# Ring tiles of 2560 instead of 2112 bytes for the left operands of a one-core decoder block, and six tiles of constants in a pool of their own

## The chip, the cores and the metric

The kernel runs on one core of one Trainium2 chip. The metric is device time in microseconds of one execution, the median of several runs. Five engines work side by side, each through its own list of instructions in order: TensorE (PE, with PEld for its weight loads), VectorE (DVE), ScalarE (ACT), GpSimd (POOL), and SyncE (SP), which issues the DMAs. They wait for each other through semaphores. SBUF is the on-chip memory from which the engines read; a tile takes the same stretch of bytes in each of 128 partitions. PSUM is where TensorE writes its sums.

## The reference

One layer of a decoder block on 1024 tokens of width 1024, in float32. What is computed, cut to what matters:

```
n    = rmsnorm(h, norm_mix)
proj = n @ w_in                      # z, xBC, dt, q, k, v, r, a1, g_ssd, g_gla: 7712 columns
y_s  = ssd_mixer(z, xBC, dt, ...)    # causal conv, chunked scan of 16 heads, gated norm
y_g  = gla_mixer(q, k, v, r, a1, ...)# gated linear attention, 4 heads, chunked
h    = h + (sigmoid(g_ssd) * (y_s @ w_up_ssd) + sigmoid(g_gla) * (y_g @ w_up_gla)) @ w_o
h    = h + cross_attention(rmsnorm(h, norm_xattn), rmsnorm(mem, norm_mem), w_xq, w_xkv, w_xo)
g, u = split(rmsnorm(h, norm_ffn) @ w_ffn_in)          # 2 x 2816 columns
h    = h + (silu(g) * u) @ w_ffn_out
out  = rmsnorm(h, norm_final)
```

## The kernel before

**Matrix products.** Each float32 operand of a large product is split into two float32r tiles, a high and a low part (`split`, L221: ACT copies to the high part, then DVE or POOL subtracts it). A product takes three matmuls per 128 rows of the contraction: high by high, high by low, low by high. Each such matmul loads 128 x 128 weights (the left, or stationary, operand) and streams 512 columns of the right, or moving, operand past them.

**Units.** The products with `w_in` and `w_ffn_in` are made in *units* of 256 columns (`Unit`, L275). A unit is one block product in the Strassen-Winograd form: seven products, named B11, B21, T1, B22, T2, T3 and T4, in place of eight. `Unit.step` (L320) makes one of the seven: it takes the left operand from the raw weights (`raw`) or a sum of them (`sa`), splits it into a pair of ring tiles `whi` and `wlo`, and issues 12 matmuls of 128 x 512 on them (L343, recorded at L51 in the helper), against the right operands `B11h`, `B11l` and so on, which hold the activations. There are 26 units on `w_in` and 22 on `w_ffn_in`: 48 x 7 x 12 = 4032 matmuls, in 21 groups of 192 by the names of their two operands.

**The ring.** `wring` (L225) gives out three pairs of tiles in turn, from the pool `wp`. Each tile holds 528 values of four bytes, 2112 bytes per partition. Of these, a unit uses 512 values: four slices (one for each k) of 128 values, so the slices are 512 bytes apart. Two other users need the ring. `kv_unit` (L549) makes keys and values of the memory tokens with 384 matmuls of 256 columns, and `v_steps` (L636) makes the columns for v, dt and a1 with 672 matmuls of 264 columns, where ring tiles are the moving operand.

**Slots.** The right operands, the raw weights and the results of units (`o`) live in *slots* of 8192 bytes: 14 in the pool `op`, 4 in `aux`, and later 4 in `m` (`open_slots`, L139). The four other large products take their left operand from a slot, too: `dense` (L1203) streams `hl` past `wd` with 1920 matmuls of 128 x 512, and the product with `w_ffn_out` (`piece`, L1596) streams `fs` past `fs`. `Att` multiplies `phl` and `kvhl`. None of these uses the ring.

**Where tiles lie.** A pool's tiles lie together. The pools opened for good lie in the order in which they are opened: constants (`cp`, L94), the ring (`wp`, L96), `op`, `aux`, and the sums `sa` (L148). Pools for a stage (`vp`, `gprep`, `conv`, `ssd`, `gla`) lie behind them, each in the place of the one that was closed. After the last of these is closed (L1133), `m`, `res` and `sa2` take their place. In the built program, the constants end at byte 9672 of the partition, the ring starts at 9696, the `op` slots at 22368, and the last tile of all ends at 229216.

**Order.** Each engine's list is fixed when the program is built. The units on `w_in` are interleaved, at rates written into the code (`run`, L438), with the steps of the SSD scan (`SSD`, L872) and then of the GLA scan (`GLA`, L1013), which are small float32 matmuls with work on ACT, DVE and POOL between them.

Of the kernel before, what the change touches and what calls it, by code (L numbers as in the profile page):

```python
# [9 lines left out]
F32 = mybir.dt.float32  # L10
F32R = mybir.dt.float32r
# [5 lines left out]
P = 128  # L17
# [4 lines left out]
MEM = 256  # L22
# [7 lines left out]
NCH = TOK // CH  # L30
NH = 16
# [47 lines left out]
def block_kernel(ctx: ExitStack, tc: tile.TileContext, t: dict, out: bass.AP):  # L79
# [10 lines left out]
    def pool(name, bufs=1, space=None, stack=None):  # L90
        kw = {"reuse_waits": "tile"} if space is None else {"space": space}
        return (stack or ctx).enter_context(tc.tile_pool(name=name, bufs=bufs, **kw))

    cp = pool("const")  # L94
    dr = pool("dram", 1, bass.MemoryType.DRAM)
    wp = pool("w", 3)  # L96
# [42 lines left out]
    def open_slots(key, n, stack):  # L139
        slots[key] = (pool(f"sl{len(slots)}{key}", n, stack=stack), n)  # L140
# [5 lines left out]
    open_slots("op", 14, opst)  # L146
    open_slots("aux", 4, auxst)
    sums = {"aux": pool("sa0", 2, stack=auxst)}  # L148

    st1 = ExitStack()  # L150
    vp = pool("vp", 1, stack=st1)
# [54 lines left out]
    def rsqrt(o, v, scale):  # L206

        DVE.tensor_scalar(o, v, scale, EPS, ALU.mult, ALU.add)
        POOL.tensor_tensor(o, o, mhalf[:, :o.shape[1]], ALU.pow)
# [13 lines left out]
        sub(e or DVE, lo, src, hi)  # L223

    def wring():  # L225
        hi = wp.tile([P, 528], F32R, name="whi", tag="whi", bufs=3)
        lo = wp.tile([P, 528], F32R, name="wlo", tag="wlo", bufs=3)
        return hi, lo

    class Operands:  # L230

# [43 lines left out]
    class Unit:  # L275
# [44 lines left out]
        def step(s, name, B, cs=ALL, again=False):  # L320
            s.load()
            kh = s.kh
            if name == "B11":
                s.banks, s.swap, s.u = {}, B.swap, False
                s.out()
            if again:
                wh, wl = s.w
            else:
                with ahead():
                    src = s.left(name)  # L330
                    hi, lo = wring()
                    s.w = wh, wl = [x[:, :kh * P].rearrange("p (k c) -> p k c", c=P) for x in (hi, lo)]
                    split(src, wh, wl)
            xh, xl = B[name]
            key = s.BANK[name]
            fresh = key not in s.banks
            if fresh:
                s.banks[key] = acc()
            p = s.banks[key]
            m = 0  # L340
            for k in range(kh):
                for x, y in ((wh, xh), (wh, xl), (wl, xh)):
                    PE.matmul(p[:, cs], x[:, k, :], y[:, k, cs], start=fresh and m == 0, stop=m == 3 * kh - 1,  # L343
                              skip_group_check=True)
                    m += 1
            s.evac(name, p, cs)
# [106 lines left out]
    def drain(g):  # L453
        for _ in g:
            pass
# [88 lines left out]
    for a in range(2):  # L544
        ACT.activation(msq, wide(mt[:, a]), AF.Square, accum_out=mss[:, a:a + 1])
    rsqrt(mss, mss, 1.0 / D)
    mbc = cp.tile([P, MEM], F32, name="mbc")

    def kv_unit(c0):  # L549

# [6 lines left out]
        for kk in range(4):  # L557
            with ahead():
                hi, lo = wring()
                hv = hi[:, :512].rearrange("p (k c) -> p k c", c=256)  # L560
                lv = lo[:, :512].rearrange("p (k c) -> p k c", c=256)
                split(raw[:, 2 * kk:2 * kk + 2, :], hv, lv, either(lo))
            for i in range(2):
                o = pa[i][:, :256]
                for k2 in range(2):
                    k = 2 * kk + k2
                    for m, (x, y) in enumerate(((hv, mh), (lv, mh), (hv, ml))):
                        w_, m_ = x[:, k2, :], y[:, k, :]
                        if c0 < D:
                            PE.matmul(o, w_[:, i * P:(i + 1) * P], m_, start=k == 0 and m == 0, stop=k == 7 and m == 2)  # L570
                        else:
                            PE.matmul(o, m_[:, i * P:(i + 1) * P], w_, start=k == 0 and m == 0, stop=k == 7 and m == 2)
            yield
# [41 lines left out]
    w_in = t["w_in"]  # L615


    dt_t = cp.tile([P, NCH, NH], F32, name="dt_t")
    a1_t = cp.tile([P, NCH, NH], F32, name="a1_t")
    HW = 264  # L620

    vraw = {}
# [13 lines left out]
    def v_steps():  # L636
        for pr in range(2):
# [13 lines left out]
            for n, name in enumerate(CHAIN):  # L651
                parts = []
                with ahead():
                    e = either(A11, 2.0)
                    if name == "T1":
                        add(e, sa, A21, A22)
                    elif name == "B22":
                        sub(e, sa, sa, A11)
                        sub(either(A11, 2.0), A12, A12, sa)
                    elif name == "T3":  # L660
                        sub(e, A21, A11, A21)
                    a = (A11, A12, sa, A12, sa, A21, A22)[n]
                    for k2 in range(2):
                        hi, lo = wring()
                        hv, lv = hi.rearrange("p (k c) -> p k c", c=HW), lo.rearrange("p (k c) -> p k c", c=HW)
                        split(a[:, 2 * k2:2 * k2 + 2, :], hv, lv)
                        parts.append((hv, lv))
# [46 lines left out]

    st2 = ExitStack()
    gp = pool("gprep", 1, stack=st2)
    cs = cp.tile([P, P], F32, name="cs")
    decays = cp.tile([P, 2 * P + 12 * NCH], F32, name="decays")
    dec, ec = decays[:, :P], decays[:, P:2 * P]
    dtv = cp.tile([P, NCH, NH], F32, name="dtv")  # L720
    ebm, ebl, ewl = (decays[:, 2 * P + i * 4 * NCH:2 * P + (i + 1) * 4 * NCH].rearrange("p (h c) -> p h c", c=NCH)
                     for i in range(3))

# [407 lines left out]
    run(singles(gs[1:] + gg[:3], B, gg[3:]), (gla, 8 * 5 / 36), prio=PRIO)  # L1131
    drain(gla)
    st4.close()  # L1133


    st5 = ExitStack()
# [112 lines left out]
    def presum():  # L1249


        r = pair[0]
        for k in range(KP):
            SP.dma_start(r, t["w_ffn_out"][256 * k:256 * k + 256, :].rearrange("(j p) c -> p j c", p=P))
            a = lambda i, j: r[:, j, half(i)]
            s1_ = sums["m"].tile([P, HALF], F32, name="sa", tag="sa", bufs=2)
            dst = down_d.rearrange("(n k p) c -> k p n c", n=4, p=P)[k]
            add(POOL, s1_, a(1, 0), a(1, 1))
            SP.dma_start(dst[:, 0], s1_)
            yield  # L1260
            sub(POOL, a(1, 1), s1_, a(0, 0))
            yield
            sub(POOL, a(1, 0), a(0, 0), a(1, 0))
            yield
            sub(POOL, a(0, 1), a(0, 1), a(1, 1))
            SP.dma_start(dst[:, 1:4], r.rearrange("p j (i c) -> p (j i) c", i=2)[:, 1:4])
            yield
# [46 lines left out]
    early = presum()  # L1314
# [299 lines left out]
    for x, (n, k, kn) in enumerate(todo):  # L1614
        name = CHAIN[n]
# [4 lines left out]
        cs = slice(0, 256) if n == 6 else ALL  # L1620
# [9 lines left out]
    cs = slice(256, 512)  # L1630
# [43 lines left out]
```

## Time and profile before

| what | time |
|---|---|
| median of 3 runs | 2018.62 us (2017.3 to 2019.04) |
| the profiled execution | 2024.24 us |
| its span, first to last instruction | 2022.5 us |
| DVE busy | 1317.2 us, 65% |
| ACT busy | 857.4 us, 42% |
| POOL busy | 673.0 us, 33% |

Stages of the program, in us from the span's start: norms, memory keys and values, and the columns for v (0 to 171); units on `w_in` (171 to 853), of which 171 to 242 go with the gates' preparation, 242 to 380 with the causal conv, 380 to about 620 with the SSD scan, and from there on with the GLA scan; the products of `dense` with cross-attention (about 870 to 1340); units on `w_ffn_in` (1353 to 1794); the product with `w_ffn_out` and the final norm (to 2022).

A line of the profile that groups instructions reads: line of the kernel, engine, operation, tile written <- tiles read, partitions x elements, count | busy time in us, mean duration of one in ns | idle time of that engine just before them, and what ended it. A matmul's recorded duration is longer than its share of the engine's time, since the next one starts before it ends; so the distance from one start to the next is the engine's busy time in a stretch divided by the matmuls in it.

### The profile page before, as it was taken

Reading aid. Unit: us, or ns where it says so; the run is one execution under the profiler, and the core shown is the slowest. Engines: PE = TensorE matmul, PEld = TensorE weight load, DVE = VectorE, ACT = ScalarE, POOL = GpSimd, SP = SyncE. Lnnn points to the kernel's source line nnn. Section 1 sums busy time; section 2 is a strip of 40 time slices with the busy share of each in tenths; the row PEclk is TensorE's granted clock in tenths of the full one; section 3 lists DMA queues with packets and bytes.
Section 4 is the critical chain, followed back from the end, with each engine's and each line's share of the span. In section 5 each row is a group of like instructions: output and inputs, shape, how many; then the busy total and the mean of one; then the engine's idle time right before and its main releaser. Section 6 shows DMA issues by size and latency. Waiting matters only on the chain.

```text
span 2022.5 us, 26282 instructions
## 1 busy us (share of the span) xinstructions
PE 1951.1 (96%) x9772; PEld 1622.4 (80%) x9772; DVE 1317.2 (65%) x1877; ACT 857.4 (42%) x1479; POOL 673.0 (33%) x500
## 2 busy tenths in 40 slices
PE   7899899999999989999999899999999999999998
PEld 6898688877788868888888688877888888888887
DVE  6864869878887656543443327478777777784565
ACT  7434645465553455532222226453333333354243
POOL 4422733455564211100044420255444444330002
PEclk9899899999999999999999999999999999999999
DMA  9332233355553745673476640333223223276463
GB/s 307 133 117 96 95 115 115 114 179 180 168 173 120 224 155 165 245 285 124 149 262 214 200 149 22 132 124 114 78 89 130 94 79 115 79 257 221 149 229 128
DMA packets 240948, 309.59 MB, mean 153 GB/s; under 512 B 16154, under 2 KB 163844, under 8 KB 240820
## 3 DMA queue, kind: packets, MB, share of 16 engines
q1 hardware_dynamic: 240820, 307.92, 45.6%
q8 instruction: 77, 1.26, 0.3%
q14 instruction: 51, 0.42, 0.1%
HBM read 211.07 MB, written 96.80 MB: 152 GB/s over the span
## 4 chain that ended last, share of the span: by engine, by line
PE 74%; DVE 8%; DMA 7%; ACT 4%; issue 3%; POOL 3%; SPq 1%; POOLq 0%; DVEq 0%; ACTq 0%
PE acc L51 65%; PE bank L51 8%; DVE wlo L73 2%; PE bank L55 1%; DMA sr<-sr_d 1%; DMA xt<-in_x_dram 1%; DMA raw<-in_w_in_dram 1%; DMA down_d<-pair 1%; DVE o L73 1%; DVE fs L73 1%; DMA fr<-act_d 1%; DMA yg_d<-sr 1%; POOL raw L73 1%; DVE y L73 1%; DMA bd<-bd_d 1%
## 5 line engine op out<-in xcount | busy, mean ns | idle before, releaser
L51 PE MATMUL acc<-hl,wd 128*128 128x512 f32 x1920 | 441.2, 391 | 7.9 <-ACT hl L1309 6.4
L51 PEld LDWEIGHTS acc<-hl,wd 128*128 128x128 f32 x1920 | 360.6, 188 | 84.2 <-ACT hl L1309 6.8
L73 DVE TENSOR_TENSOR wlo<-raw,whi 128x512 fp32r<-128x512 f32 x264 | 246.3, 937 | 73.1 <-ACT whi L222 72.7
L222 ACT ACTIVATE whi<-raw 128x512 fp32r<-128x512 f32 x272 | 170.0, 629 | 261.6 <-PE acc L51 221.2
L73 DVE TENSOR_TENSOR o<-acc,o 128x512 f32<-128x512 f32 (+1 forms) x256 | 172.8, 676 | 123.1 <-PE acc L51 110.6
L51 PE MATMUL acc<-fs 128*128 128x512 f32 (+1 forms) x792 | 156.0, 356 | 1.4 <-ACT o L1569 1.3
L51 PEld LDWEIGHTS acc<-fs 128*128 128x128 f32 x792 | 130.6, 189 | 22.5 <-ACT o L1569 1.7
L73 POOL TENSOR_TENSOR raw<-raw,sa 128x512 f32<-128x512 f32 x46 | 61.2, 1330 | 246.6 <-DVE wlo L73 243.6
L222 ACT ACTIVATE fs<-fr 128x1024 fp32r<-128x1024 f32 (+1 forms) x84 | 80.0, 984 | 112.9 <-PE acc L51 38.7
L73 DVE TENSOR_TENSOR fs<-fr,fs 128x1024 fp32r<-128x1024 f32 (+1 forms) x84 | 99.7, 1218 | 38.6 <-ACT fs L222 38.0
L222 ACT ACTIVATE whi<-sa 128x512 fp32r<-128x512 f32 x96 | 60.0, 627 | 107.9 <-PE acc L51 107.5
L73 POOL TENSOR_TENSOR sa<-pair 128x512 f32<-128x512 f32 x11 | 15.3, 1393 | 255.4 <-DVE pair L73 178.9
L73 POOL TENSOR_TENSOR sa<-raw 128x512 f32<-128x512 f32 x46 | 71.1, 1545 | 85.4 <-DMA raw<-in_w_in_dram 47.6
L73 DVE TENSOR_TENSOR wlo<-sa,whi 128x512 fp32r<-128x512 f32 x96 | 83.1, 866 | 18.4 <-ACT whi L222 18.3
L222 ACT ACTIVATE wd<-raw 128x1024 fp32r<-128x1024 f32 x40 | 42.3, 1058 | 92.0 <-PE acc L51 87.6
L73 POOL TENSOR_TENSOR o<-o 128x512 f32<-128x512 f32 x29 | 49.2, 1703 | 91.5 <-DVE o L73 78.2
L51 PE MATMUL acc<-T2h,wlo 128*128 128x512 f32 x192 | 76.8, 400 | 3.0 <-DVE wlo L73 3.0
L51 PE MATMUL acc<-B22h,wlo 128*128 128x512 f32 x192 | 77.8, 405 | 1.8 <-DVE wlo L73 1.8
L51 PE MATMUL acc<-B21h,whi 128*128 128x512 f32 x192 | 77.1, 402 | 2.4 <-ACT o L352 2.4
L73 POOL TENSOR_TENSOR raw<-raw 128x512 f32<-128x512 f32 x46 | 78.2, 1701 | 3.0 <-DVE sa L73 3.0
L51 PE MATMUL acc<-T2h,whi 128*128 128x512 f32 x192 | 76.7, 400 | 2.5 <-ACT whi L222 2.5
L51 PE MATMUL acc<-T3h,wlo 128*128 128x512 f32 x192 | 77.1, 401 | 1.5 <-DVE wlo L73 1.5
(373 smaller groups left out, 4845.2 us busy)
## 6 DMA issues: line engine op xcount, KB each, us to landing
raw<-in_w_in_dram SPq DMA_DIRECT2D x26, 1024.0 KB, 5.6
raw<-in_w_ffn_in_dram SPq DMA_DIRECT2D x22, 1024.0 KB, 6.9
act_d<-o SPq DMA_DIRECT2D x77, 256.0 KB, 2.0
fr<-act_d SPq DMA_DIRECT2D x35, 512.0 KB, 4.8
pair<-in_w_ffn_out_dram SPq DMA_DIRECT2D x11, 1024.0 KB, 5.1
fr<-down_d SPq DMA_DIRECT2D x20, 512.0 KB
down_d<-pair SPq DMA_DIRECT2D x11, 768.0 KB
raw<-in_w_xkv_dram SPq DMA_DIRECT2D x8, 1024.0 KB
```

Source lines behind the costliest of these rows:

```text
L51: return s.e.matmul(o, x, y, **kw)
L55: return s.e.transpose(o, x, i)
L73: return f(*a, **kw)
L222: ACT.activation(hi, src, AF.Copy)
```

## The change

The ring tiles become 640 values wide, 2560 bytes, of which the first 528 are used as before. To make room, six tiles of constants that nothing reads after the GLA scan (`mbc`, `dt_t`, `a1_t`, `cs`, `decays`, `dtv`; 4480 bytes together) move from the pool of constants to a new pool `early`. It lies behind `sa`, below the pools of the stages, and is closed with the GLA scan's pool, so that `m` takes its place.

```diff
+    st_early = ExitStack()
+    ep = pool("early", 1, stack=st_early)
...
     def wring():
-        hi = wp.tile([P, 528], F32R, name="whi", tag="whi", bufs=3)
-        lo = wp.tile([P, 528], F32R, name="wlo", tag="wlo", bufs=3)
-        return hi, lo
+
+        return [wp.tile([P, 640], F32R, name=n, tag=n, bufs=3)[:, :528] for n in ("whi", "wlo")]
...
-    mbc = cp.tile([P, MEM], F32, name="mbc")
+    mbc = ep.tile([P, MEM], F32, name="mbc")
...
-    dt_t = cp.tile([P, NCH, NH], F32, name="dt_t")
-    a1_t = cp.tile([P, NCH, NH], F32, name="a1_t")
+    dt_t = ep.tile([P, NCH, NH], F32, name="dt_t")
+    a1_t = ep.tile([P, NCH, NH], F32, name="a1_t")
...
-    cs = cp.tile([P, P], F32, name="cs")
-    decays = cp.tile([P, 2 * P + 12 * NCH], F32, name="decays")
+    cs = ep.tile([P, P], F32, name="cs")
+    decays = ep.tile([P, 2 * P + 12 * NCH], F32, name="decays")
...
-    dtv = cp.tile([P, NCH, NH], F32, name="dtv")
+    dtv = ep.tile([P, NCH, NH], F32, name="dtv")
...
     drain(gla)
     st4.close()
+    st_early.close()
```

Every engine has the same instructions as before in the same order. In the built program the constants now end at byte 5192, the ring starts at 5216, the `op` slots at 20576, and the last tile ends at 227424. What differs is where tiles lie, and a few waits at the first tiles of the pools that are opened after the GLA scan: ACT and DVE wait for one DMA less before the first `wd` tile is split, and POOL waits for the same things in another grouping before the first `sa` tile of `sa2`.

## The prediction

> **What bounds the kernel now.** I first read the head of the page: the span, the busy shares, the granted clock, and the shares of the chain that ended last.
>
> ```profile
> span 2022.5 us, 26282 instructions
> PE 1951.1 (96%) x9772; PEld 1622.4 (80%) x9772; DVE 1317.2 (65%) x1877; ACT 857.4 (42%) x1479; POOL 673.0 (33%) x500
> ...
> PEclk9899899999999999999999999999999999999999
> ...
> PE 74%; DVE 8%; DMA 7%; ACT 4%; issue 3%; POOL 3%; SPq 1%; POOLq 0%; DVEq 0%; ACTq 0%
> ```
>
> TensorE is busy for 1951.1 of 2022.5 us, at full clock nearly throughout, and the chain of waits lies on it for 74%. So the question is what one matmul costs. The groups of equal instructions give a first hint (count | busy time, mean ns of one):
>
> ```profile
> L51 PE MATMUL acc<-hl,wd 128*128 128x512 f32 x1920 | 441.2, 391 | 7.9 <-ACT hl L1309 6.4 <-DVE wd L73 0.8 <-ACT wd L222 0.6
> L51 PE MATMUL acc<-fs 128*128 128x512 f32 x528 | 122.5, 391 | 1.3 <-ACT o L1569 1.3
> ...
> L51 PE MATMUL acc<-B22h,wlo 128*128 128x512 f32 x192 | 77.8, 405 | 1.8 <-DVE wlo L73 1.8
> L51 PE MATMUL acc<-B11l,whi 128*128 128x512 f32 x192 | 75.6, 394 | 0.0
> ```
>
> All four are 128x512 matmuls on float32r operands with a new load of weights each. Those with both operands in slots (`hl` with `wd`, `fs` with `fs`) are recorded with 391 ns, the slowest and the fastest groups on ring tiles with 405 and 394. Recorded durations overlap, so I read the distance from start to start out of busy times by stretch (columns: stretch, its length, then busy us and count for PE, PEld, DVE, ACT, POOL, then granted clock, DMA share, GB/s):
>
> ```profile
> core 0: us, PE busy (x) PEld busy (x) DVE busy (x) ACT busy (x) POOL busy (x), PEclk, DMA share, GB/s
> 900.00:1060.00 160.00, 160.00 (x707) 132.48 (x707) 68.94 (x85) 45.15 (x63) 21.92 (x16) 1.00 0.50 173
> 1400.00:1700.00 300.00, 300.00 (x1296) 243.19 (x1296) 223.84 (x278) 101.24 (x172) 138.44 (x95) 1.00 0.31 104
> 250.00:300.00 50.00, 50.00 (x217) 40.52 (x216) 32.61 (x36) 23.79 (x35) 20.43 (x22) 1.00 0.34 112
> 300.00:350.00 50.00, 50.00 (x216) 40.10 (x215) 45.10 (x48) 26.50 (x34) 16.03 (x9) 1.00 0.34 116
> ```
>
> The first stretch holds nothing on PE but `dense` (slots against slots), the others nothing but units (ring against slots). PE is never idle in any of them, and the clock is 1.00. One matmul takes 160/707 = 226.3 ns of PE in `dense`, and 300/1296 = 231.5 ns, 50/217 = 230.4 and 50/216 = 231.5 ns in units. The counts include one or two matmuls that reach over a stretch's edges, which makes the short stretches look faster; with 1.7 taken off each count the long ones give 226.9 and 231.8. I take **5.0 ns more for a matmul on ring tiles**.
>
> What makes the difference? Not the neighbours: within the two conv stretches DVE goes from 65% to 90% busy and POOL from 41% to 32%, and the units stay at 231. `dense` and the units have the same shape, the same order of operands (high-high, high-low, low-high) and the same load of weights per matmul. What they don't share is where operands lie. Slots are 8192 bytes and lie one behind another, slices in them are at multiples of 512 bytes, so in `dense` left and right operands are always a multiple of 512 bytes apart. A ring tile of 2112 = 4 x 512 + 64 bytes shifts each next tile by 64, and the ring's six tiles end 24 x 512 + 384 bytes behind its start, where the slots begin: the six lie 384, 320, 256, 192, 128 and 64 bytes off a multiple of 512, never 0. The trace has no ring tile at 0, so that the offset is the cause is inferred; but it is the one difference left.
>
> **The change part by part.** *The ring.* 2560 = 5 x 512, and six tiles are 15360 = 30 x 512, so every one of the 4032 unit matmuls gets operands a multiple of 512 apart, as `dense` has. If each then takes 5.0 ns less, PE is relieved of 4032 x 5.0 = 20.2 us. Which part of this reaches the end is read from the chain of waits in each stretch with units, in order 171.3 to 242, 242 to 380, 380 to 700, 700 to 853.2, and 1352.6 to 1794 us:
>
> ```profile
> by line: PE acc L51 39.5%; DVE wlo L73 8.8%; ACT gy L792 6.4%; ACT gy L798 6.1%; ACT whi L222 4.7%; issue 4.4%; ACT L467 3.6%; ACT gy L777 3.5%; DVE raw L73 3.0%; DVE gy L73 2.9%; ACT gx L776 2.9%; PE bank L51 2.8%; DVE sa L73 2.5%; POOL ra
> ...
> by line: PE acc L51 100.1%
> ...
> 241.83 138.18 PE acc L51 x587
> ...
> by line: PE acc L51 35.9%; PE bank L51 8.6%; issue 7.5%; DMA raw<-in_w_in_dram 4.9%; DVE wlo L73 3.8%; DVE y L73 3.3%; POOL raw L73 3.0%; POOL y L73 2.7%; POOL sa L73 2.4%; DMA bd<-bd_d 2.4%; ACT e L911 2.1%; DVE o L73 2.0%; DVE csb L73 1.6
> ...
> by line: PE acc L51 37.5%; DMA sr<-sr_d 13.2%; PE bank L51 12.5%; DMA yg_d<-sr 7.4%; issue 5.1%; PE bank L55 3.7%; DMA qk<-q_d 3.0%; ACT L1082 2.5%; DVE sr L73 2.3%; POOL ss L73 2.1%; DMA bd<-bd_d 1.9%; ACT o L1076 1.6%; ACT o L1079 1.4%; D
> ...
> by line: PE acc L51 91.8%; issue 1.8%; DVE fs L73 1.2%; DVE T4l L73 1.1%; DVE T2l L73 1.1%; DVE wlo L73 0.8%; PE bank L51 0.6%; DVE diag L73 0.3%; ACT fs L222 0.2%; DVE o L73 0.2%; DVE ssum L73 0.2%; ACT o L1464 0.2%; DVE ga L73 0.1%; DVE B
> ```
>
> The chain's part on unit matmuls ("PE acc L51") is 39.5% of 70.7 us = 27.9; all 138.2; 35.9% of 320 = 114.9; 37.5% of 153.2 = 57.5; 91.8% of 441.4 = 405.2. Each of these shrinks by 5.0/231.5 = 2.16%: 0.6 + 3.0 + 2.5 + 1.2 + 8.8 = **16.1 us**. While the scans run, more than half of the chain goes through DVE, ACT, POOL and DMAs, though PE is nearly always busy; there a faster matmul mostly lengthens PE's short waits. What is late next in that place is the scan's own step (`y`, `csb`, `sr`), which no part of the change touches.
>
> *The other users of the ring.* With mh and ml, the 384 matmuls of 256 columns go to offset 0, too. The nearest rows, durations as minimum/median/maximum in ns:
>
> ```profile
> L51 PE MATMUL acc<-kvhl,hl x192: 274/283/387, 1211.0 to 1252.3; 128*128 128x256 f32 x192
> ...
> L51 PE MATMUL bank<-mh,wlo x64: 274/280/386, 74.4 to 113.9; 128*128 128x256 f32 x64
> L51 PE MATMUL acc<-wlo,mh x48: 275/282/394, 11.4 to 34.9; 128*128 128x256 f32 x48
> ```
>
> At offset 0 (`kvhl` with `hl`) the median is 283, on ring tiles 280 and 282. So no gain shows at this length: between -5 and +3 ns x 384, that is 1.9 us less to 1.2 us more, and as these stages wait for loads much of the time, I take 0.3 us more. For the 672 matmuls of 264 columns half the slices go to 0 and half to 32 bytes off; nearest are the same rows, the bounds are -3.4 to +2.0 us, and I take 0.
>
> *Splits.* ACT and DVE write the ring tiles and read the raw weights at other offsets from each other.
>
> ```profile
> L73 DVE TENSOR_TENSOR wlo<-raw,whi x264: 659/691/2900, 10.6 to 1784.9; 128x512 fp32r<-128x512 f32 x132
> ...
> L73 DVE TENSOR_TENSOR fs<-fr,fs x84: 673/1217/2325, 1779.4 to 1991.1; 128x1024 fp32r<-128x1024 f32 x70, 128x512 fp32r<-128x512 f32 x14
> ```
>
> The splits into ring tiles have offsets other than 0 against `raw`, those of `fs` have 0, and the shortest of 512 columns take 659 and 673 ns: no faster at 0. The bound is 14 ns more on each of 360 splits, 5 us of DVE beside busy matmuls, of which the chain's 0.8% on `wlo` in the FFN's units lets next to nothing through. I take 0.
>
> *The constants and the pools behind them.* All tiles of the scans shift by the same amount against each other, but by another one against the constants (`ident`, `ones`, `triu`), which some 430 small float32 matmuls and transposes use. No row shows such pairs at two offsets; with the 5.0 ns of the large ones as price, it is -2.2 to +2.2 us if all were on the chain. The rows of the scans put 8.6% and 12.5% of the chain on "PE bank L51", so I take 0 and keep plus or minus 0.3.
>
> *The waits at the first `wd`.* ACT and DVE wait for one DMA less.
>
> ```profile
> L222 ACT ACTIVATE wd<-raw 128x1024 fp32r<-128x1024 f32 x6 | 6.4, 1059 | 13.1 <-PE acc L51 12.4 <-DMA raw<-in_w_up_ssd_dram 0.7
> ```
>
> ACT's first six `wd` splits are preceded by 12.4 us of waits for PE and 0.7 for the load of weights, and none for a store: nothing to gain, at most the 0.7. No engine gets a wait that it did not have, and every engine's list has its old order, so nothing queues behind a new one.
>
> *The sum.* 16.1 - 0.3, with 0.2 off for the waits that PE still meets among the units of the FFN, is 15.6 us. The profiled execution, 2024.24 us, would become 2008.6. It lies 5.6 us (0.3%) over the median of the runs; scaling the gain to the median would change it by 0.04 us, so I take the same 15.6 off the median: **2003.0 us**. Around it: 13 to 18 us, 2000.6 to 2005.6.
>
> [...]
>
> **The rivals.** Three more rows bear on them: the two stretches with the scans, in the columns above, and PE's waits for `wlo` in the whole span (us in total, times, longest).
>
> ```profile
> 380.00:700.00 320.00, 311.00 (x1802) 252.82 (x1801) 253.57 (x440) 160.04 (x332) 148.76 (x114) 0.99 0.55 171
> 700.00:853.20 153.20, 144.86 (x683) 119.53 (x683) 90.11 (x173) 77.42 (x157) 28.03 (x23) 0.98 0.56 181
> ...
> PE acc L51 <- DVE wlo L73: 8.5, 7, 3.0
> ```
>
> *All of it reaches the end.* The chain is inferred from semaphores, and PE is busy for 311.00 of 320 us in the scans' first stretch as well; if the scan's steps move up with the matmuls, the gain is the whole 20.2 us minus 0.3: 1998.7. Against it stand the DMA and DVE pieces in the chain from 380 on. *Only the pure stretches gain.* If the first stretch and the scans give back everything, 3.0 + 8.8 - 0.5 = 11.3 us are left: 2007.3. For it: PE's share of the chain there is below 40%. *The offset is not the cause.* Something else keeps matmuls on the ring at 231.5 ns, for instance that ACT and DVE have just written the tiles that PE reads next. Then nothing moves but the small terms: 2018.6, plus or minus 2. [...] Against it: `wd` is written in the same way, in two tiles by turns, and takes 226.3. *Slower.* The splits run on DVE while POOL works, and of the 264 `wlo<-raw,whi` the median takes 691 ns, the longest 2900, so some may meet POOL and take 1 us and more beyond the usual. PE's pace moves the two against each other. Among the scans stand the 16 units on r, q, k and the two gates, 1344 matmuls in 112 steps of 12; a step lasts 12 x 231.5 = 2.8 us, and a split that is late by more than its lead stops PE. If 40 more of the 112 splits came 1 us late with PE waiting, that costs 40 us, 24 more than the gain: 2043. It turns slower from 16 late ones on. Against it: PE waits for `wlo` on unit matmuls 7 times now, 8.5 us in all, and the order of steps stays.
>
> **How the numbers follow.** Forecast (2000.6 to 2005.6) 0.58, all of it 0.20, only the pure stretches 0.11, not the cause 0.07, slower 0.04. The range from 1998 to 2009 takes in the first three, 0.89 less their edges, and the bounds of the small terms. Faster by over 0.2% (4 us, about what a measurement of this kernel can tell from no change) is 0.89, within it 0.07, slower 0.04.
>
> **What would show it.** In the FFN's units, a stretch of 300 us without waits holds some 1325 matmuls instead of 1296, and the groups on ring tiles come down to about 391 ns, all alike. From the first unit of the FFN to the last, about 9 us are gone; from 242 to 380, 3; from 380 to 853, less than the 6.7 that 1344 matmuls would give, with PE's waits longer there. The 256-column rows and the splits stay. The prediction is wrong if the groups stay at 394 and over (the offset is not it), or if they fall and the span doesn't (the chain is elsewhere), or if stretches without units change by more than 2 us.

## The result and the profile after

The changed kernel takes 2008.84 us (median of 6 runs, 2006.89 to 2013.24), against 2020.10 us before (median of 6). The ratio is 0.9947, 95% interval 0.9934 to 0.9960: 10.7 us less, 8.1 to 13.3. The forecast was 15.6 us less, with 13 to 18 around it. So the sign is right and a third of the gain did not arrive.

The head of the page of the changed kernel:

```profile
span 2006.7 us, 26281 instructions
PE 1934.2 (96%) x9772; PEld 1622.0 (81%) x9772; DVE 1320.9 (66%) x1877; ACT 855.7 (43%) x1479; POOL 675.2 (34%) x500
...
PEclk9899899999999999999999999999999999999999
...
PE 68%; DVE 11%; DMA 7%; ACT 4%; issue 4%; POOL 4%; SPq 1%; POOLq 0%; DVEq 0%; ACTq 0%
```

The chain of waits lies on PE for 68% now, 74% before; VectorE's share went from 8 to 11%. Next the stretches from which the prediction read the cost of a matmul (stretch, length, then busy us and count for PE, PEld, DVE, ACT, POOL, then granted clock, DMA share, GB/s), and the groups on ring tiles, first over the whole span and then in the FFN's units alone:

```profile
900.00:1060.00 160.00, 160.00 (x707) 132.55 (x706) 70.70 (x85) 44.01 (x62) 23.54 (x16) 1.00 0.52 176
1400.00:1700.00 300.00, 300.00 (x1325) 248.47 (x1325) 230.12 (x283) 101.11 (x174) 143.53 (x96) 1.00 0.30 101
250.00:300.00 50.00, 50.00 (x222) 41.44 (x221) 32.47 (x37) 24.36 (x36) 21.87 (x22) 1.00 0.35 113
300.00:350.00 50.00, 49.38 (x215) 39.86 (x215) 45.08 (x48) 25.58 (x35) 15.29 (x9) 1.00 0.34 116
```

```profile
L51 PE MATMUL acc<-hl,wd 128*128 128x512 f32 x1920 | 440.8, 391 | 5.7 <-ACT hl L1311 5.6
...
L51 PE MATMUL acc<-B22h,wlo 128*128 128x512 f32 x192 | 77.2, 402 | 3.0 <-DVE wlo L73 3.0
L51 PE MATMUL acc<-B11l,whi 128*128 128x512 f32 x192 | 74.9, 390 | 0.0
...
L51 PE MATMUL acc<-B22h,wlo 128*128 128x512 f32 x64 | 24.9, 389 | 0.0
```

In the FFN's units 300 us hold 1325 matmuls instead of 1296: 226.4 ns each instead of 231.5, and `dense` is where it was (160/707 = 226.3). The expected size, 5.0 ns, is the measured one, 5.1. The second window in the conv tells of trouble, though: the first one has 222 matmuls instead of 217 in 50 us, the second 215, with PE idle for 0.62 us of it, where before it had 216 and no idle time.

The other rows that the prediction named, duration as minimum/median/maximum in ns:

```profile
L51 PE MATMUL bank<-mh,wlo x64: 277/283/387, 74.5 to 114.1; 128*128 128x256 f32 x64
L51 PE MATMUL acc<-wlo,mh x48: 282/283/385, 11.1 to 34.7; 128*128 128x256 f32 x48
...
L73 DVE TENSOR_TENSOR wlo<-raw,whi x264: 659/692/2835, 10.4 to 1769.0; 128x512 fp32r<-128x512 f32 x132
```

The 256-column matmuls have a median of 283 ns, 3 and 1 ns more than before and the same as `kvhl` with `hl` at offset 0; the splits stay.

Where the time went is read by cutting each trace at the starts of the same five instructions: the first and the last conv tap on VectorE, the first and the last `dense` matmul, and the last `acc<-B11l,whi`. With two more traces of each kernel, from runs of the first and the last group of experiments below, in us:

| stretch | before (3 traces) | changed (3 traces) | difference of means |
|---|---|---|---|
| start to first tap | 286.9, 288.8, 291.4 | 286.2, 287.1, 287.0 | 2.3 |
| first to last tap (conv) | 109.2, 109.2, 109.2 | 109.2, 109.1, 109.1 | 0.1 |
| last tap to first `dense` (scans) | 451.7, 447.9, 451.7 | 447.9, 448.9, 449.1 | 1.8 |
| first to last `dense` | 504.6, 501.8, 498.9 | 502.0, 501.0, 502.2 | 0.0 |
| to the last `acc<-B11l,whi` (FFN units) | 421.5, 421.3, 421.3 | 412.8, 412.9, 412.9 | 8.5 |
| to the end | 248.6, 250.8, 249.2 | 248.6, 248.7, 248.7 | 0.9 |

Two rows are exact: the FFN's units give 8.5 us, and between the taps of the conv nothing is gained. The others vary from trace to trace by as much as they differ. The sum of the differences, 13.5 us, is more than the runs show, because the three profiled executions of before (2024.24, 2021.52 and 2023.33 us) lie 2.3 to 5.6 us over the medians of the runs beside them.

### The profile page after: what moved, and what is told of

The parts are those of the page before. It is cut to its first block, busy times and chain, and to the rows that moved or that the text cites. A ratio compares the mean times of both kernels' runs of the same rounds, so it can differ in the third digit from the quotient of the medians.

```text
span 2006.7 us, 26281 instructions
## 1 busy us (share of the span) xinstructions
PE 1934.2 (96%) x9772; PEld 1622.0 (81%) x9772; DVE 1320.9 (66%) x1877; ACT 855.7 (43%) x1479; POOL 675.2 (34%) x500
## 4 chain that ended last, share of the span: by engine, by line
PE 68%; DVE 11%; DMA 7%; ACT 4%; issue 4%; POOL 4%; SPq 1%; POOLq 0%; DVEq 0%; ACTq 0%
PE acc L51 60%; PE bank L51 7%; DVE wlo L73 3%; DVE cv L73 2%; DVE o L73 1%; DMA sr<-sr_d 1%; DMA xt<-in_x_dram 1%; PE bank L55 1%; DMA yg_d<-sr 1%; DMA raw<-in_w_in_dram 1%; POOL sa L73 1%; DMA csb<-cs_d 1%; DMA down_d<-pair 1%; POOL ssum L73 1%; DMA fr<-act_d 1%
## 5 line engine op out<-in xcount | busy, mean ns | idle before, releaser
L51 PE MATMUL acc<-B22h,whi 128*128 128x512 f32 x192 | 76.3, 398 | 1.3 <-ACT o L468 1.3
```

The lines of the kernel that those rows point to most:

```text
L51: return s.e.matmul(o, x, y, **kw)
```

## The experiments

**Is it where the operands lie?** Theory: the distance between left and right operand sets the pitch of the unit matmuls. Rivals: the moved constants and pools, or the larger tiles as such. Both kernels were run again beside two variants. The first has the constants in their new pool and the old ring:

```diff
-        return [wp.tile([P, 640], F32R, name=n, tag=n, bufs=3)[:, :528] for n in ("whi", "wlo")]
+        return [wp.tile([P, 528], F32R, name=n, tag=n, bufs=3) for n in ("whi", "wlo")]
```

The second keeps the changed kernel's tiles and starts 256 bytes later in each, so that no tile moves:

```diff
-        return [wp.tile([P, 640], F32R, name=n, tag=n, bufs=3)[:, :528] for n in ("whi", "wlo")]
+        return [wp.tile([P, 640], F32R, name=n, tag=n, bufs=3)[:, 64:592] for n in ("whi", "wlo")]
```

Before again, expected:

> The kernel before, unchanged, for a second profile and the spread from run to run. Both theories: same time as before, ratio 1.000 within 0.002, and some 1296 matmuls in a 300 us stretch of FFN units. What differs between this trace and the first one of before (2024.24 us, 5.6 over its median) outside the units is run-to-run spread; I expect up to 4 us of it at PE's waits in the scans and in the dense products near 1120 us.

Changed again, expected:

> The changed kernel, unchanged, for a second profile. Ratio to before 0.9947 within 0.002 as in the first measurement; 1325 matmuls in 300 us of FFN units. If the gain is the FFN's units' 9 us plus what the first part lets through, the stretch 241 to 398 us again gains only about 1 us over before, not 3.

Constants alone, expected:

> The six constants moved to the early pool, the ring tiles left at 2112 bytes: left and right operands are 64 to 384 bytes off a multiple of 512, as before. Theory (the offset sets the pitch of matmuls): 1296 matmuls in 300 us of FFN units, time as before, ratio 0.998 to 1.002. Rival (the moved constants and pools bring the gain): 1296 as well but the time near 2009, ratio 0.995.

256 bytes later, expected:

> The changed kernel, where each ring tile of 2560 bytes is used from byte 256 on, so that no tile moves and only the distance of left to right operands goes from 0 to 256 bytes modulo 512, for all 4032 unit matmuls. Theory (offset): the pitch goes back to 231 to 234 ns, 1283 to 1300 matmuls in 300 us of FFN units, ratio to before 0.997 to 1.003. Rival (larger tiles, or pools in other places, bring the gain): 1325 matmuls, ratio 0.995.

Measured as ratios to before: before again 0.9998 (0.9984 to 1.0012), changed again 0.9960 (0.9945 to 0.9975), constants alone 1.0009 (1.0000 to 1.0018), 256 bytes later 0.9947 (0.9935 to 0.9959). The 300 us of FFN units, in this order:

```profile
1400.00:1700.00 300.00, 300.00 (x1296) 243.20 (x1295) 226.16 (x277) 100.56 (x172) 140.52 (x95) 1.00 0.31 101
```

```profile
1400.00:1700.00 300.00, 300.00 (x1325) 248.43 (x1324) 230.37 (x283) 101.01 (x173) 142.36 (x96) 1.00 0.31 102
```

```profile
1400.00:1700.00 300.00, 300.00 (x1296) 243.24 (x1295) 225.35 (x278) 100.79 (x172) 138.30 (x94) 1.00 0.32 104
```

```profile
1400.00:1700.00 300.00, 300.00 (x1326) 248.39 (x1325) 229.04 (x284) 100.76 (x173) 143.16 (x96) 1.00 0.31 101
```

The constants alone bring nothing: 1296 matmuls. But the miss is the last one: at 256 bytes off the matmuls are as fast as at 0, where the theory had them back at 231 to 234 ns. So "a multiple of 512" is not what counts. Before had a distance of 256 for one of its six tiles, and no group of its matmuls was fast.

**What must hold, then?** Two theories fit: C, the distance must not change from one matmul to the next; M, every distance must be a multiple of 256 bytes. Four variants of the changed kernel, by the lines that differ: `wlo` alone 256 bytes later; both 64 bytes later; a pair of tiles in one of 9 x 512 + 64 bytes, which the profile names `whi` throughout; slices 528 bytes apart.

```diff
+        return [wp.tile([P, 640], F32R, name="whi", tag="whi", bufs=3)[:, :528],
+                wp.tile([P, 640], F32R, name="wlo", tag="wlo", bufs=3)[:, 64:592]]
...
+        return [wp.tile([P, 640], F32R, name=n, tag=n, bufs=3)[:, 16:544] for n in ("whi", "wlo")]
...
+        w = wp.tile([P, 1168], F32R, name="whi", tag="whi", bufs=3)
+        return w[:, :528], w[:, 640:]
...
+                    s.w = wh, wl = [x[:, :kh * 132].rearrange("p (k c) -> p k c", c=132)[:, :, :P] for x in (hi, lo)]
```

`wlo` alone, expected:

> The changed kernel with whi used from byte 0 of its tile and wlo from byte 256, so the distance from left to right operand is 0, 0, 256 in turn over each three matmuls. Since a constant 256 turned out as fast as 0, two theories are left. C: what counts is that the distance stays the same from one matmul to the next. Then this kernel falls back to 230 to 233 ns, 1290 to 1305 matmuls in 300 us of FFN units. M: what counts is that every distance is a multiple of 256 bytes. Then it stays at 226.7 ns, 1325 matmuls.

Both 64 bytes later, expected:

> The changed kernel with both ring tiles used from byte 64 on: every distance is 64 bytes off a multiple of 512 (448 modulo 512), and the same for all. C (a constant distance): 226.7 ns, 1325 matmuls in 300 us of FFN units. M (multiples of 256): 230 to 235 ns, 1280 to 1305.

Pairs, expected:

> The ring of the changed kernel as three tiles of 4672 bytes, 9 x 512 + 64, each holding the high part at byte 0 and the low part at byte 2560: within a product of 12 matmuls the distance is the same, from one product to the next it moves by 64 bytes or by 128 back. C: 11 of 12 steps are as with a constant distance, 1318 to 1325 matmuls in 300 us of FFN units. M: distances of 64, 128 and 192, none a multiple of 256, 1285 to 1305.

Slices 528 bytes apart, expected:

> The changed kernel with the four slices of a ring tile 528 instead of 512 bytes apart, so the distance is 0, 496, 480, 464 modulo 512 over k, the same for the three matmuls of one k. C: every third step has a change of 16 bytes; between the constant case and before, 1305 to 1322 matmuls in 300 us of FFN units. M: three of four distances are no multiple of 256, 1285 to 1308.

The FFN's units of the four, in this order:

```profile
1400.00:1700.00 300.00, 300.00 (x1325) 248.47 (x1325) 230.28 (x284) 101.12 (x173) 142.26 (x96) 1.00 0.31 102
```

```profile
1400.00:1700.00 300.00, 300.00 (x1287) 240.42 (x1286) 220.59 (x276) 99.56 (x169) 136.98 (x94) 1.00 0.32 105
```

```profile
1400.00:1700.00 300.00, 300.00 (x1295) 242.71 (x1294) 222.54 (x279) 101.30 (x171) 138.81 (x94) 1.00 0.31 105
```

```profile
1400.00:1700.00 300.00, 300.00 (x1295) 243.44 (x1294) 224.48 (x276) 100.39 (x171) 141.12 (x95) 1.00 0.30 101
```

M holds in all four and C in none: a distance that jumps between 0 and 256 costs nothing (1325), a constant one of 64 is slower than before (1287, 233.1 ns). The times, one run each, were 2009.88, 2029.54, 2033.86 and 2019.32 us.

Two more runs follow. Both tiles 128 bytes later (`[:, 32:560]`), and 64 bytes more among the constants, so that both operands move together:

```diff
+    cp.tile([P, 16], F32, name="shift")
```

128 bytes later, expected:

> The changed kernel with both ring tiles used from byte 128 on: every distance is 128 bytes off a multiple of 256. If multiples of 256 are what counts: slower, 1283 to 1305 matmuls in 300 us of FFN units. If multiples of 128 do, too: 1325.

Both operands moved, expected:

> The changed kernel with 64 bytes more at the end of the constants, so ring, slots and all that lies behind move by 64 bytes together and the distances stay multiples of 512. If the distance between the operands counts: 1325 matmuls in 300 us of FFN units and 707 in 160 us of dense. If each operand's own address counts (until now all fast cases had both at 96 bytes over a multiple of 256): slower, below 1305 and below 700.

The FFN's units, in this order:

```profile
1400.00:1700.00 300.00, 300.00 (x1288) 241.38 (x1287) 222.84 (x275) 99.64 (x169) 140.24 (x95) 1.00 0.30 101
```

```profile
1400.00:1700.00 300.00, 300.00 (x1325) 248.39 (x1325) 229.41 (x284) 101.55 (x175) 141.72 (x95) 1.00 0.31 104
```

At 128 it is as slow as at 64 (1288, 2020.98 us); moved together they are fast (1325, and 708 of `dense` in 160 us; 2011.24 us). So it is the distance of the two operands to each other, not the address of either, and of the distances tried only multiples of 256 bytes are fast.

**Where did the conv's 3.0 us go?** Theory: VectorE, 45.10 of 50 us busy in the conv, was right behind PE and takes the gain back. In both kernels one of the conv's taps was left out (m = 0, 12 instructions; that part of the conv is not computed):

```diff
-            for m in range(3):
+            for m in range(1, 3):
```

Before without the tap, expected:

> The kernel before with one of the causal conv's three taps on VectorE left out (the part m = 0 of the conv isn't computed, 12 instructions of about 1.3 to 1.6 us). The conv's stretch was paced by PE, so it lasts as long as before: from the first to the last unit matmul of it within 1 us of the 156 us that it takes in the two traces of before.

Changed without the tap, expected:

> The changed kernel with the same tap of the conv left out. Theory: in the conv's stretch VectorE, 90% busy, takes back what the matmuls gain, which is why it got only 1 us shorter and not 3; relieved of the tap it lets the gain through, and the stretch is 2.5 to 3.2 us shorter than in the kernel before without the tap. Rival (something else than VectorE's conv work holds PE there, such as loads of weights): it is 0.5 to 1.3 us shorter, as with all taps.

Measured between the starts of the same two unit matmuls in each trace, 624 matmuls apart (249.5 and 394.5 us in the first trace of before; the second lies ahead of the SSD scan's first matmul in every trace), before takes 145.1 us in all three traces with all taps, and 144.6 without one, as expected (the 156 us of the expectations span 672 matmuls). The changed kernel takes 144.0 in all three, and 141.4 without the tap. So the gain is 1.1 us with all taps and 3.2 without one, as the theory has it. (Most of the 1.1 lies ahead of the first tap at 287 us, where VectorE has no conv work yet: hence the 0.1 in the table.) The chain in that stretch shows why, first of the changed kernel (241 to 398 us), then of the changed kernel and of before without the tap (245 to 395 us):

```profile
by line: PE acc L51 40.3%; DVE cv L73 19.6%; DVE wlo L73 15.2%; DVE o L73 9.0%; issue 7.0%; ACT cv L731 4.0%; ACT cv L736 2.9%; ACT whi L224 2.0%; DVE sa L73 0.4%; DVEq L73 0.1%; ACTq L731 0.1%; ACTq L736 0.1%
```

```profile
by line: PE acc L51 88.3%; DVE cv L73 3.3%; DMA csb<-cs_d 3.2%; DMA xbc_d<-cv 2.0%; DVE o L73 0.9%; ACT cv L731 0.8%; ACT cv L736 0.7%; DVE wlo L73 0.6%; SPq L889 0.5%; issue 0.3%; ACTq L731 0.0%; ACTq L736 0.0%
```

```profile
by line: PE acc L51 100.3%
```

With all taps, PE has 40% of the chain and VectorE's `cv`, `wlo` and `o` 44% together, where before PE had all of it. Without a tap PE has 88% again, the rest from 377 us on, and 300 to 350 us hold 222 matmuls instead of 215:

```profile
300.00:350.00 50.00, 50.00 (x222) 41.39 (x222) 36.22 (x43) 27.40 (x36) 16.73 (x10) 1.00 0.31 110
```

Was VectorE behind PE, or level with it? From 300 to 378.2 us, four rounds of a unit's 84 matmuls, first of before, then of the changed kernel:

```profile
300.00:378.20 78.20, 78.20 (x337) 62.82 (x336) 71.67 (x73) 40.04 (x52) 29.55 (x17) 1.00 0.32 108
```

```profile
300.00:378.20 78.20, 77.38 (x337) 62.74 (x337) 71.67 (x73) 39.22 (x53) 29.53 (x17) 1.00 0.32 108
```

Both kernels get through the same 337 matmuls, with VectorE busy for the same 71.67 us. So before was held at VectorE's pace here already, though its PE shows no idle time. A matmul is recorded with 391 ns and the next starts after 231, so a delay of up to about 160 ns leaves no gap in the record, and busy time divided by matmuls counts it as pitch. The single matmuls of one round show it (start and length in us, and in brackets idle time and what ended it), again before first:

```profile
301.86 0.48 PE L51 MATMUL acc<-B22h,wlo 128*128 128x512 f32 x1
302.18 0.40 PE L51 MATMUL acc<-B22h,whi 128*128 128x512 f32 x1
```

```profile
300.51 0.39 PE L51 MATMUL acc<-B22l,whi 128*128 128x512 f32 x1
301.11 0.50 PE L51 MATMUL acc<-B22h,wlo 128*128 128x512 f32 x1 [0.21 <-DVE wlo L73]
301.45 0.40 PE L51 MATMUL acc<-B22h,whi 128*128 128x512 f32 x1
```

Before has one long step per round here, 0.32 us in place of 0.23. The changed kernel has two, 0.60 and 0.34, and the first is a wait for VectorE's `wlo`. The round takes 19.6 us in both. Without the tap no such step is left in either, and a round takes 19.5 us in before and 19.0 in the changed kernel.

**Can the conv's part be had?** The tap m = 0 is multiplied on ScalarE and added on GpSimd, so all is computed; the changed kernel and before were run once more beside it.

```diff
+                if m == 0:
+                    x = cvp.tile([P, TOK], F32, name="cx", tag="cx", bufs=2)
+                    ACT.activation(x[:, s_:], row[:, :TOK - s_], AF.Copy, scale=tap(m))
+                    add(POOL, c[:, s_:], c[:, s_:], x[:, s_:])
```

Tap on two other engines, expected:

> The changed kernel with one of the conv's three taps taken off VectorE: ScalarE multiplies it, GpSimd adds it. All is computed. If VectorE's conv work is what takes the gain back, the conv's stretch is 1.5 to 3.5 us shorter than in the changed kernel (153.5 us or less instead of 155.3), and the ratio to before is 0.993 to 0.995. Rival (ScalarE's and GpSimd's part now delays the next steps of the conv, or the splits): the conv's stretch is as long as in the changed kernel or longer, ratio 0.995 to 0.998.

Changed, a third time, expected:

> The changed kernel again. Ratio to before 0.9945 to 0.996; the scans' stretch (398 us to the first dense matmul) 447 to 451 us, 1 to 3 us less than the mean over the traces of before, not the 3.7 of the prediction.

Before, a third time, expected:

> The kernel before again, for a third trace: the conv's stretch 156.3 us as in the others, the scans' stretch 449 to 453 us.

The rival came true: ratio 0.9981 (0.9969 to 0.9993) against 0.9949 (0.9934 to 0.9965) for the changed kernel beside it, 111.4 us from the first to the last tap on VectorE, and 146.5 us for the 624 matmuls instead of 144.0. In 300 to 350 us:

```profile
300.00:350.00 50.00, 49.29 (x211) 38.56 (x210) 45.42 (x51) 28.36 (x38) 14.33 (x6) 1.00 0.36 120
```

VectorE is busy for 45.42 us, no less than the 45.08 with all taps, though it has a third fewer of them; GpSimd's new additions (`cv<-cv,cx`, median 2410 ns) run beside it. The trace shows two reasons. The program gives each addition of a unit to GpSimd or VectorE by its own estimate of which is free first (`either`), and beside GpSimd's new work it gave VectorE 23 of them instead of 6 (`sa<-raw`, `sa<-sa,raw` and `raw<-raw`), at some 0.68 us each. And VectorE's taps of 1022 columns got longer: 2248 ns on average from 288 to 395 us, against 1637 in the changed kernel beside it. So this run did not try a conv with a third less work on VectorE; whether that would win the 2 us stays open, and so does what makes the taps longer. No version faster than the changed kernel was found.

## Why the prediction was right in kind and too large

- **The price of a matmul** was right: 5.0 ns forecast, 5.1 measured in the FFN's units (231.5 to 226.4).
- **Its cause** was half right. That the place of the operands sets it is shown: the same tiles used from byte 0 or 256 give 1325 and 1326 matmuls in 300 us, from byte 64 or 128 1287 and 1288. That it takes a multiple of 512 was too narrow; 256 does.
- **The FFN's units** were forecast with 8.8 us, less 0.2 at the sum: 8.5 measured.
- **The conv** is the step that failed: "all 138.2" us of chain on PE were given 3.0 us, and 1.1 came. The prediction took a PE without idle time and a chain of 100% on PE for a stretch that PE paces. The runs showed VectorE level with it: a round of 84 matmuls takes 19.6 us in both kernels, and with one tap less the gain is 3.2 us. The row that said so was quoted in the prediction, 45.10 of 50 us busy on VectorE, and was used only to show that neighbours don't slow matmuls. A chain names the one that came last; it doesn't say by how much, and a PE whose records overlap (391 ns long, 231 from start to start) hides short waits.
- **The scans** were given 2.5 + 1.2 = 3.7 us; the means of three traces differ by 1.8, with 3.8 between traces of the same kernel. So the term was probably too large, but by how much, and why, the runs don't settle. PE is idle longer there, as was foreseen: 17.3, 15.5 and 17.1 us from the last tap to the first `dense` matmul in before, 18.9, 20.2 and 17.8 in the changed kernel. The two waits that grew most in the first traces (us in total, times, longest), first of before, then of the changed kernel:

```profile
PE bank L51 <- DVE y L73: 2.0, 3, 1.3
PE bank L51 <- DVE S L73: 1.0, 1, 1.0
```

```profile
PE bank L51 <- DVE y L73: 4.6, 3, 2.4
PE bank L51 <- DVE S L73: 2.7, 1, 2.7
```

- **The stretch of 171 to 242 us** was given 0.6. It lies in the first row of the table, where traces of before differ by 4.5 us; nothing can be said of it.
- **The small terms** held: 256-column matmuls 1 to 3 ns slower, splits and `dense` unchanged, and no new wait at the first `wd` splits (12.2 us for PE and 0.4 for the load of weights, instead of 12.4 and 0.7).

With 1.1 for the conv, 1.8 for the scans and 8.5 for the FFN, these three terms give 11.4 us in place of 15.5 (3.0 + 3.7 + 8.8), and with the 0.6 and the 0.3 off as forecast 11.7; the interval of 8.1 to 13.3 holds both. Of the rivals, the one in which only the pure stretches gain (11.3 us, 2007.3) came nearest in time, but by luck: one of its two pure stretches was the one that failed.

In these runs the same instructions on the same tiles take 226.4 ns (changed kernel) or 233.1 ns (64 bytes later) by distance alone. By what means the distance acts was not shown. Nor do the runs tell whose distance counts: that of the matmul's own weights, or of the next one's, whose load, 188 ns long, is recorded beside it.

## What to carry to other kernels

Here float32r matmuls of 128x512 that each load their own weights took 226.2 to 226.4 ns where the distance between left and right operand was a multiple of 256 bytes for all buffers of the ring, and 231.5 to 233.1 ns in the runs where it wasn't. So check that distance; a tile size that isn't a multiple, such as the 2112 bytes of before (231.5 ns), makes the buffers drift. Before counting a faster engine's gain, look at the second busiest engine in each stretch by itself: at 90% busy, in turn with the first, it kept back 2.1 of 3.2 us here. Don't take a PE without idle time for one that never waits: look at the steps from start to start (one of 0.32 us among those of 0.23 here). And measure pitch in a stretch without waits: it agreed there in every trace (1295 or 1296, and 1325 or 1326, matmuls), while the spans of one kernel's three traces differed by 0.1%, 2 to 3 us.

## What the hardware did that was not expected

- A good distance didn't help a matmul among others with bad ones. By starts in the traces, before's matmuls on the ring tile at 256 bytes take 231 ns (the six tiles 231 to 234), and those of the slices 528 bytes apart that lie at 0 take 232; both distances give 226.8 where all are multiples of 256.
- A multiple of 256 bytes was enough: 226.2 ns at 256 (300/1326), 226.4 at 0 and with a distance that jumps between 0 and 256 from matmul to matmul (300/1325).
- A constant distance of 64 or 128 bytes off was slower (233.1 and 232.9 ns) than the drifting distances of before (231.5). The one run of the variant with 64 bytes, 2029.54 us, is 6.5 us over the mean of the three profiled executions of before, as much as the units' pitch makes (4032 x 1.6 ns). That of the one with pairs, 2033.86 us, is 10.8 over it; cut like the table's traces, it loses 7.7 us ahead of the first tap and 4.1 in the scans. Its pitch is about that of before (1295 matmuls in 300 us), so what makes these is open.
- At 256 columns a distance of 0 brought nothing: recorded medians of 283 ns against 280 and 282.
